# Two FFN units planned with the mixer, and the FFN's normalised activations moved from VectorE to ScalarE and GpSimd

## The chip, the core and the metric

The kernel runs on one core of one Trainium2 chip. The metric is the device time of one execution in microseconds (us), as the median of several runs. Five engines work side by side, each with its own queue of instructions that is worked off in order: TensorE (PE, with its weight loads shown apart as PEld), VectorE (DVE), ScalarE (ACT), GpSimd (POOL) and SyncE (SP, which here issues the DMAs).

## What is computed

Two pre-normalised residual layers and a last norm, for 512 tokens of width 1024. Layer 0's mixer has stick-breaking and native-sparse attention heads, layer 1's has forgetting attention. Each layer ends in a gated MLP (called FFN below) with a causal convolution of width 3 over its activation branch, and 2816 hidden channels:

```python
def rmsnorm(x, g):
    x32 = x.astype(jnp.float32)
    y = x32 * lax.rsqrt(jnp.mean(x32 * x32, axis=-1, keepdims=True) + NORM_EPS)
    return y.astype(x.dtype) * g

def conv_glu_ffn(h, w_in, conv_w, conv_b, w_out):
    a, b = jnp.split(h @ w_in, 2, axis=-1)
    a = conv(a, conv_w) + conv_b          # causal, width 3, each channel by itself
    return (jax.nn.silu(a) * b) @ w_out

for layer in range(DEPTH):
    x = x + mixer(rmsnorm(x, attn_norm[layer]))
    x = x + conv_glu_ffn(rmsnorm(x, ffn_norm[layer]), ...)
return rmsnorm(x, final_norm)
```

## The kernel before

All activations lie transposed, with channels on the 128 partitions and the 512 tokens along the free dimension, so X is eight tiles X[0] to X[7]. Each fp32 operand is split in a high part and a low part, and a product of 128 input channels is three matmuls: high weights by high activations, low weights by high activations, high weights by low activations. The weights are split on the fly: a DMA brings the tile wraw, ScalarE copies it to whi (rounding it), and VectorE subtracts, giving wlo. The pairs whi and wlo have two buffers each, and so has wraw.

**A mixer's end.** The last output projections add their products to X (VectorE, line 541). For each finished X[m], Mixer.feed (line 545) gives the FFN's input: ScalarE makes XH[m] = X[m] times the norm's gain g, VectorE makes the low part XL[m], ScalarE squares X[m], and GpSimd adds the square to ACC. The factor 1/rms (tile rstd) is left out of XH and XL. It is known only when all of ACC is, and it is multiplied in when a product is taken out of PSUM.

**An FFN's start** (ffn, line 1121). A unit is 128 of the columns of w_in: eight steps of three matmuls, one step for each XH[k], XL[k]. The first six column pairs (PLAIN = 6, so twelve units) are plain: for pair c, unit 2c gives the activation branch a, unit 2c+1 gives b. VectorE takes a and b out of PSUM with a product by rstd, makes two of the convolution's three taps, the product by silu, and the low part GL of the result; ScalarE makes the first tap, silu, and the high part GH. norm() makes rstd: a matmul of ACC with ones (written below as stats), then VectorE, ScalarE twice and VectorE three times.

The other 16 pairs go by a scheme with seven products in place of eight (function seven, tiles named s, t and o in PSUM). It needs sums and differences of normalised activations, which sums(k) makes for k = 0 to 3: VectorE writes x[k] = X[k] * g * rstd and x[k+4] likewise (line 1245, tile gh), GpSimd makes four half-wide sums d1 and d3 from them (tile gl), and ScalarE and VectorE split them into b1, b2, t1 and t3. No product of seven can start before all of these are there.

**What sets the order.** A mixer and an FFN are each written as a list of jobs for a planner (class Plan, line 104). A job has an engine, a cost in us written by hand, jobs it depends on, a priority, and buffers that it takes and gives back. The planner simulates the engines with those costs: of the jobs of an engine that could start within 0.03 us of the earliest, the one with the lowest priority number goes first. The order that comes out is each engine's program order, and nothing on the chip changes it. On VectorE, taking products out of PSUM has priority 1, gates 1.1, weight splitting 1.2, sums 2 to 2.3 and XL 4. A unit's matmuls have 100 and more.

The mixer's plan ends with its last projection. After it, ffn issues the weights of its first two units (line 1131, outside of the plan) and starts a second plan whose engines come free at times written by hand (line 1132). In that plan unit 0 runs to its end, the matmul stats is issued behind unit 0's seventh step (lines 1222 and 1223), and unit 1 follows. Plain units alternate between two PSUM banks (mm_bank), and two more banks, t and o, are kept for the sevens.

Of the kernel before, what the change touches and what calls it, by code (L numbers as in the profile page):

```python
# [10 lines left out]
F32 = mybir.dt.float32  # L11
# [7 lines left out]
P = 128  # L19
# [74 lines left out]

class Job:


    def __init__(self, eng, cost, fn, deps, prio, take, give, lat):
        self.eng, self.cost, self.fn, self.deps = eng, cost, fn, deps
        self.prio, self.take, self.give, self.lat = prio, take, give, lat  # L100
        self.end, self.got = None, []


class Plan:
# [13 lines left out]
    def add(self, eng, cost, fn, *deps, prio=5.0, take=(), give=(), lat=0.0):  # L118
        j = Job(eng, cost, fn, [d for d in deps if d is not None], prio, take, give, lat)
        self.jobs.append(j)  # L120
        return j

    def _when(self, j):
# [8 lines left out]
        for n in set(j.take):  # L132
            b = sorted(self.bufs[n])[:j.take.count(n)]
            if len(b) < j.take.count(n):
                return None
            t = max(t, b[-1][0] + self.LAG)
        return t

    def run(self):
        while self.jobs:  # L140
# [14 lines left out]
            for n in j.take:  # L155
# [5 lines left out]
            for n in j.give:  # L161

                for n, i in [(n, 0)] if isinstance(n, str) else [g for g in n.got if g[0] == "b"]:
# [6 lines left out]
def trunk(ctx, tc, A):  # L170
# [17 lines left out]
    names = dict(t=2, o=3)  # L188
# [5 lines left out]
    def hand_over(plan):  # L194

        order = [i for _, i in sorted(plan.bufs["b"])]
        turns.clear()
        turns.extend(order[:2])
        names.update(t=order[2], o=order[3])
# [52 lines left out]
    def warm():  # L252
# [3 lines left out]
        ps = bank(names["t"], "t")  # L256
# [94 lines left out]
    def finish(fp, src, oh, ol):  # L351
# [48 lines left out]
        for b in range(2):  # L400
            for m in ms:
                tag = ("mm", "mm", "t", "o")[m - ms[0]]
                ps = mm_bank() if tag == "mm" else bank(names[tag], tag)
# [42 lines left out]
    class Mixer:  # L446


        def __init__(self, plan, qp, ap):
            self.plan, self.qp, self.ap = plan, qp, ap  # L450
            self.seq, self.prev_load, self.prev_v = 0, None, None
            self.copied = [None, None]
            self.vs = []

        def bank(self, name, n=0):
            return bank([i for k, i in self.plan.now.got if k == "b"][n], name)
# [88 lines left out]
        def feed(self, m, layer, j):  # L545
# [15 lines left out]
            def scaled():  # L561
# [4 lines left out]
            self.plan.add("DVE", 0.75, lambda: dve.scalar_tensor_tensor(XL[m], X[m], g, XH[m].bitcast(F32), op0=ALU.mult, op1=ALU.subtract),  # L566
                          a, prio=4)
            a = self.plan.add("ACT", 0.62, square, j, prio=4.5, take=("sq",))
            self.plan.add("POOL", 1.35, add, a, prio=4, give=("sq",))
# [232 lines left out]
    def layer0():  # L802
        with ExitStack() as es:
# [71 lines left out]
            def new_o():  # L875
                o = bank(names["o"], "o")
# [233 lines left out]
            part(range(4, 8), 6, 2, (oj[7],), last)  # L1110
            inorder[0] = True
            plan.run()
            inorder[0] = False
            hand_over(plan)
# [6 lines left out]
    def ffn(layer, nl, final):  # L1121
# [7 lines left out]
        with ExitStack() as es:  # L1129
            fp = es.enter_context(tc.tile_pool(name=f"fp{layer}", bufs=2))  # L1130
            first = [weights(A["wfi"][layer, u], [P, NK, P]) for u in range(2)]
            plan = Plan(dict(PE=0.0, ACT=2.6, DVE=2.6, POOL=4.9, SP=-5.0), dict(PE=0.03), wraw=2, wb=2, wo=2, w=2, mm=2, s=2, t=1, o=1,
                        a=2, tt=1, b=2, g=10, sr=2, slot=NK, sq=2)
            plan.bufs["w"], plan.bufs["slot"] = [], []
# [34 lines left out]
            def gated(c, box, *deps):  # L1169
# [7 lines left out]
                GJ[c] = add("DVE", 0.69, lambda: dve.tensor_sub(GL[c], box["b"], GH[c].bitcast(F32)), j, prio=p, give=("b",))  # L1177


            def norm():  # L1180
# [12 lines left out]
                acc = add("POOL", 0.0, lambda: None, prio=0)  # L1193
                j = add("PE", 0.5, stats, acc, prio=0, take=("s",))
# [10 lines left out]
            def plain(c, root):  # L1205
                box = {}
                ps = []
                for u in range(2):
                    w = M.weights(A["wfi"][layer, 2 * c + u], [P, NK, P]) if c else (dict(h=first[u][0], l=first[u][1]), None)
                    lastu = (c, u) == (PLAIN - 1, 1)  # L1210
                    bx, j = {}, None
                    for k in range(NK):
                        def step(k=k, w=w, bx=bx):
                            if k == 0:
                                bx["ps"] = mm_bank()
# [17 lines left out]
                j = add("DVE", 0.69, fa, ps[0][1], root[0], prio=1, take=("a",), give=("mm",))  # L1233
# [447 lines left out]
```

## Time and profile before

| what | value |
|---|---|
| median of 3 runs | 1252.84 us (1252.83 to 1253.6) |
| the profiled execution's own time | 1250.37 us |
| its span in the profile | 1248.2 us |
| TensorE busy | 1223.1 us, 98% of the span |
| VectorE, ScalarE, GpSimd busy | 923.0, 631.6 and 230.2 us |
| first FFN's matmuls begin, sevens begin | 289.78 us, 360.55 us |
| second FFN's matmuls begin, sevens begin | 882.10 us, 951.53 us |

A row of the timeline has the start, the duration in us, the engine, the operation, the tile written and the tiles read, the shape, and how often it comes in a row; in brackets stands how long the engine sat idle before it and who ended that. Durations of neighbours overlap by some hundredths, so the distance between starts is what an instruction costs its engine. All instructions go through one helper (L88), so they are told apart by tile names.

### The profile page before, as it was taken

The page shows a single profiled execution, that of the slowest core. Times are in us where ns is not written, and L with a number is a line of the kernel's source. Part 1 is how long each engine was busy: PE and PEld are TensorE (multiplying, and loading weights), DVE is VectorE, ACT ScalarE, POOL GpSimd, SP SyncE. Part 2 cuts the span into 40 slices and gives each one's busy share as a digit, 9 for nine tenths or more (in the row PEclk, how much of TensorE's full clock was granted, in tenths as well). Part 3 has the DMA queues.
Part 4 walks back from the last instruction along what each step waited for, and adds up shares of the span by engine and source line. Part 5 has one row for each costly group of instructions (what it writes and reads, how often), then busy time and mean ns, then how long its engine had stood idle before and what let it go on. Part 6 is the DMA issues. An engine that isn't in the chain of part 4 may idle for free.

```text
span 1248.2 us, 19483 instructions
## 1 busy us (share of the span) xinstructions
PE 1223.1 (98%) x7484; PEld 1038.2 (83%) x7484; DVE 923.0 (74%) x1576; ACT 631.6 (51%) x1148; POOL 230.2 (18%) x272
## 2 busy tenths in 40 slices
PE   8999999999999999999999999999999999999997
PEld 5887866677889999999887878777788999999986
DVE  6668757658998799888762443444899889988875
ACT  6676537745554445444452664542555445444452
POOL 0000104413510001000030452310441000100011
PEclk9999999999999999999999999999999999999999
DMA  6314141012251342323233553312225124232421
GB/s 213 118 35 124 52 130 52 18 51 83 86 169 41 113 132 81 114 72 137 78 109 105 188 160 98 110 52 85 85 86 168 64 94 148 72 108 82 131 66 68
DMA packets 51420, 124.18 MB, mean 99 GB/s; under 512 B 6064, under 2 KB 17584, under 8 KB 51328
## 3 DMA queue, kind: packets, MB, share of 16 engines
q1 hardware_dynamic: 49808, 121.35, 30.0%
q10 hardware_dynamic: 1520, 1.59, 0.4%
q8 instruction: 59, 0.97, 0.3%
q14 instruction: 33, 0.27, 0.1%
HBM read 119.28 MB, written 2.13 MB: 97 GB/s over the span
## 4 chain that ended last, share of the span: by engine, by line
PE 88%; DVE 6%; ACT 1%; issue 1%; SPq 1%; DMA 1%; POOL 1%; DVEq 0%; ACTq 0%; POOLq 0%
PE mm L88 50%; PE s L88 20%; PE t L88 10%; PE o L88 7%; SPq L88 1%; DVE x L88 1%; DVE xl L88 1%; DVE wlo L88 1%; POOL e L88 1%; DVE e L88 1%; ACT whi L88 0%; DMA x<-x 0%; DVE sxl L88 0%; ACT xh L88 0%; DMA swp<-q 0%
## 5 line engine op out<-in xcount | busy, mean ns | idle before, releaser
L88 PE MATMUL mm<-xl,whi 128*128 128x512 f32 x424 | 166.2, 392 | 5.0 <-DVE xl L88 4.9
L88 PE MATMUL mm<-xh,whi 128*128 128x512 f32 x424 | 169.5, 400 | 1.4 <-ACT xh L88 1.4
L88 PE MATMUL mm<-xh,wlo 128*128 128x512 f32 x424 | 165.7, 391 | 1.1 <-DVE wlo L88 1.1
L88 DVE TENSOR_TENSOR wlo<-wraw,whi 128x1024 fp32r<-128x1024 f32 (+3 forms) x83 | 105.8, 1275 | 55.0 <-ACT whi L88 54.7
L88 ACT CAST whi<-wraw 128x1024 fp32r<-128x1024 f32 (+3 forms) x83 | 83.8, 1010 | 99.3 <-PE mm L88 73.8
L88 POOL TENSOR_TENSOR sr<-wraw,wb 128x512 f32<-128x512 f32 x32 | 47.4, 1481 | 462.8 <-DVE sr L88 288.1
L88 PE MATMUL mm<-gh,wlo 128*128 128x512 f32 x332 | 130.1, 392 | 0.0
L88 PE MATMUL mm<-gh,whi 128*128 128x512 f32 x332 | 130.0, 392 | 0.0
L88 PE MATMUL mm<-gl,whi 128*128 128x512 f32 x332 | 129.2, 389 | 0.0
L88 ACT CAST sxh<-sr 128x512 fp32r<-128x512 f32 x128 | 76.4, 617 | 83.5 <-DVE sr L88 54.2
L88 DVE TENSOR_TENSOR x<-x,mm 128x512 f32<-128x512 f32 (+2 forms) x104 | 70.0, 674 | 63.9 <-PE mm L88 63.5
L88 PEld LDWEIGHTS mm<-xl,whi 128*128 128x128 f32 x424 | 79.8, 188 | 24.6 <-DVE xl L88 7.5
L88 POOL TENSOR_SCALAR e<-e,dn 128x128 f32<-128x128 f32 (+3 forms) x128 | 72.3, 586 | 148.7 <-DVE dn L88 148.6
L88 PEld LDWEIGHTS mm<-xh,whi 128*128 128x128 f32 x424 | 79.9, 189 | 21.4 <-issue 3.3
L88 DVE TENSOR_TENSOR sxl<-sr,sxh 128x512 fp32r<-128x512 f32 x128 | 95.0, 760 | 2.7 <-ACT sxh L88 1.9
L88 PEld LDWEIGHTS mm<-xh,wlo 128*128 128x128 f32 x424 | 80.0, 189 | 18.1 <-DVE wlo L88 1.7
L88 ACT ACTIVATE tt<-a,conv 128x512 f32<-128x512 f32 x44 | 36.0, 817 | 114.5 <-DVE a L88 114.5
L88 ACT ACTIVATE e<-e,nm 128x256 f32<-128x256 f32 (+3 forms) x128 | 70.8, 556 | 43.9 <-DVE nm L88 40.9
L88 DVE SCALAR_TENSOR_TENSOR tt<-a,conv,tt 128x510 f32<-128x510 f32 x88 | 72.6, 826 | 8.4 <-ACT tt L88 7.2
L88 PEld LDWEIGHTS mm<-gl,whi 128*128 128x128 f32 x332 | 62.4, 188 | 13.3
L88 PE MATMUL s<-t3l,sxh 128*128 128x256 f32 x256 | 72.4, 283 | 0.0
L88 PE MATMUL s<-t3h,sxl 128*128 128x256 f32 x256 | 72.4, 283 | 0.0
(248 smaller groups left out, 3372.4 us busy)
## 6 DMA issues: line engine op xcount, KB each, us to landing
wraw<-wfi SPq DMA_DIRECT2D x56, 512.0 KB
wb<-wfi SPq DMA_DIRECT2D x32, 512.0 KB
wraw<-wu SPq DMA_DIRECT2D x31, 512.0 KB
wo<-wfo SPq DMA_DIRECT2D x32, 384.0 KB
wo<-wfo SPq DMA_DIRECT2D x28, 320.0 KB
wraw<-wo SPq DMA_DIRECT2D x16, 512.0 KB
wraw<-wv SPq DMA_DIRECT2D x10, 512.0 KB
cb<-cd SPq DMA_DIRECT2D x8, 512.0 KB
```

What stands on the lines that cost most here:

```text
L88: r = f(*a, **k)
```

## The change

1. **Two units in the mixer's plan.** ahead(M, layer), called behind the last projections and before the mixer's plan runs, adds the weights and the steps of the FFN's units 0 and 1 as jobs. Each step depends on the job that makes XL[k]. Their priority, 100 and the running number of their weights, lies behind that of the projections.
2. **What is handed over.** hand_over() passes on when each engine, weight buffer and PSUM bank comes free in the mixer's plan and when ACC is complete, and the FFN's plan starts from these. It no longer contains units 0 and 1; stats is its first matmul, so it comes behind both units.
3. **Banks.** Units 0 and 1 keep the banks they had in the mixer's plan. The plain units after them take whichever of the four (mm, t, o) comes free first.
4. **The normalised activations.** x[c] = X[c] * g is made by ScalarE, which needs no rstd, and GpSimd multiplies it by rstd in place. VectorE does nothing for it. x[k+4] is scaled only after x[k] has been multiplied.
5. The written cost of GpSimd's add to ACC goes from 1.35 to 1.4 us.

```diff
+    def ahead(M, layer):
+        first = []
+        for u in range(2):
+            w = M.weights(A["wfi"][layer, u], [P, NK, P])
+            bx, j = {}, None
+            for k in range(NK):
+                def step(k=k, w=w, bx=bx):
+                    if k == 0:
+                        bx["ps"] = M.bank("mm")
+                    h, l = w[0]["h"][:, k], w[0]["l"][:, k]
+                    mm(bx["ps"], h, XH[k], k == 0, False)
+                    mm(bx["ps"], l, XH[k], False, False)
+                    mm(bx["ps"], h, XL[k], False, k == NK - 1)
+                j = M.plan.add("PE", 0.69, step, w[1], M.xl[k], j, prio=100 + M.seq, take=("b",) if k == 0 else (), give=("w",) if k == NK - 1 else ())
+                bx.setdefault("job", j)
+            first.append((bx, j))
+        return first
...
-            first = [weights(A["wfi"][layer, u], [P, NK, P]) for u in range(2)]
-            plan = Plan(dict(PE=0.0, ACT=2.6, DVE=2.6, POOL=4.9, SP=-5.0), dict(PE=0.03), wraw=2, wb=2, wo=2, w=2, mm=2, s=2, t=1, o=1,
-                        a=2, tt=1, b=2, g=10, sr=2, slot=NK, sq=2)
-            plan.bufs["w"], plan.bufs["slot"] = [], []
+            plan = Plan(left["free"], dict(PE=0.03), wb=2, wo=2, s=2, a=2, tt=1, bb=2, g=10, sr=2, sq=2)
+            plan.bufs.update(w=left["w"], wraw=left["wraw"], slot=[], mm=[], t=left["b"][:1], o=left["b"][1:])
...
-                acc = add("POOL", 0.0, lambda: None, prio=0)
-                j = add("PE", 0.5, stats, acc, prio=0, take=("s",))
+                j = add("PE", 0.5, stats, left["acc"], prio=0, take=("s",))
...
-                        j = add("PE", 0.685, step, w[1], j, prio=100 + c, take=("mm",) if k == 0 else (), give=give)
-                        if (c, u, k) == (0, 0, NK - 2):
-                            root.append(next(nj))
+                        j = add("PE", 0.685, step, w[1], j, prio=100 + c, give=give, alts=("mm", "t", "o") if k == 0 else ())
...
                 def norm(c):
                     x[c] = g_tile("gh", F32)
-                    dve.scalar_tensor_tensor(x[c], X[c], ng[:, nl - 1, c:c + 1], rstd, op0=ALU.mult, op1=ALU.mult)
+                    act.activation(x[c], X[c], AF.Copy, scale=ng[:, nl - 1, c:c + 1])
...
-                j = add("DVE", 0.75, lambda: norm(k), root[0], prio=p, take=("g",))
-                j = add("DVE", 0.75, lambda: norm(k + H), j, prio=p, take=("g",))
-                eng, e, cost = (pool, "POOL", 0.74) if True else (dve, "DVE", 0.42)
+                eng, e, cost = pool, "POOL", 0.74
+                j = None
+                for c in (k, k + H):
+                    j = add("ACT", 0.73, lambda c=c: norm(c), j, prio=p, take=("g",))
+                    j = add(e, 1.4, lambda c=c: eng.tensor_mul(x[c], x[c], rstd), j, root[0], prio=p)
```

More of the change, by code (lines that the diff above doesn't have):

```diff
@@ L116, in __init__, with add @@
         self.jobs = []
-    def add(self, eng, cost, fn, *deps, prio=5.0, take=(), give=(), lat=0.0):
-        j = Job(eng, cost, fn, [d for d in deps if d is not None], prio, take, give, lat)
+    def add(self, eng, cost, fn, *deps, prio=5.0, take=(), give=(), lat=0.0, alts=()):
+        j = Job(eng, cost, fn, [d for d in deps if d is not None], prio, take, give, lat, alts)
         self.jobs.append(j)
@@ L136, in _when @@
             t = max(t, b[-1][0] + self.LAG)
+        if j.alts:
+            b = [(min(self.bufs[n]), n) for n in j.alts if self.bufs[n]]
+            if not b:
+                return None
+            j.choice = min(b)[1]
+            t = max(t, min(b)[0][0] + self.LAG)
         return t
@@ L154, in run @@
             self.jobs.remove(j)
-            for n in j.take:
+            for n in (*j.take, j.choice) if j.alts else j.take:
                 b = min(self.bufs[n])
@@ L192, in mm_bank, with done, hand_over @@
         return bank(turns[-1], "mm")
[L194 to L199, printed above, removed]
+    left = {}
+    def done(t):
+        j = Job("", 0.0, None, [], 0, (), (), 0.0)
+        j.end = t
+        return j
+    def ahead(M, layer):
[15 more added lines that the diff above has]
+        return first
+    def hand_over(M, first):
+        plan = M.plan
+        t = plan.free["PE"]
+        left["free"] = {e: f - t for e, f in plan.free.items()}
+        left["acc"] = done(M.acc.end - t)
+        left["w"] = [(f - t, i) for f, i in plan.bufs["w"]]
+        left["wraw"] = [(f - t, i) for f, i in plan.bufs["wraw"]]
+        left["b"] = sorted((f - t, i) for f, i in plan.bufs["b"])
+        left["first"] = []
+        for bx, j in first:
+            d = done(j.end - t)
+            d.got = [("mm", i) for n, i in bx["job"].got if n == "b"]
+            left["first"].append((dict(bx, job=d), d))
     def s_banks():
@@ L255, in warm @@
         pool.memset(z, 0.0)
[L256 removed]
+        ps = bank(2, "t")
         for n in range(12):
@@ L452, in __init__ @@
             self.copied = [None, None]
+            self.xl, self.acc = {}, None
             self.vs = []
         def bank(self, name, n=0):
-            return bank([i for k, i in self.plan.now.got if k == "b"][n], name)
+            return bank([i for k, i in self.plan.now.got if k in BANKS][n], name)
         def weights(self, src, shape, place=None, token="w", split=None):
@@ L1113, in layer0 @@
             inorder[0] = False
-            hand_over(plan)
+            hand_over(M, first)
     layer0()
@@ L1208, in plain @@
                 for u in range(2):
-                    w = M.weights(A["wfi"][layer, 2 * c + u], [P, NK, P]) if c else (dict(h=first[u][0], l=first[u][1]), None)
+                    if c == 0:
+                        ps.append(left["first"][u])
+                        continue
+                    w = M.weights(A["wfi"][layer, 2 * c + u], [P, NK, P])
                     lastu = (c, u) == (PLAIN - 1, 1)
@@ L1345, in seven @@
                 j = product(1, "p2", "t2", "t")
-                u = take("DVE", 0.42, first_b, j, cp_, take=("b",), give=("t",))
+                u = take("DVE", 0.42, first_b, j, cp_, take=("bb",), give=(j,))
                 j = product(2, "p1", "t1", "s")
@@ L1349, in seven @@
                 j = product(3, "p4", "b22", "o")
-                c12 = take("DVE", 0.42, lambda: dve.tensor_sub(av(HI), box[3], bv(HI)), j, v, give=("o",))
+                c12 = take("DVE", 0.42, lambda: dve.tensor_sub(av(HI), box[3], bv(HI)), j, v, give=(j,))
                 j = product(4, "p3", "t3", "s")
@@ L1353, in seven @@
                 j = product(5, "a2", "b21", "t")
-                c11 = take("DVE", 0.42, lambda: dve.tensor_add(av(LO), av(LO), box[5]), j, u, give=("t",))
+                c11 = take("DVE", 0.42, lambda: dve.tensor_add(av(LO), av(LO), box[5]), j, u, give=(j,))
                 t = gate(c, box, c11, c12)
@@ L1582, in layer1 @@
             inorder[0] = False
-            hand_over(plan)
+            hand_over(M, first)
     layer1()
```

38 lines of the change are left out of this document (21 added, 17 removed).

## The prediction

> **What bounds the kernel now.** I read the page first: busy times, then the chain of work that ended last.
>
> ```profile
> span 1248.2 us, 19483 instructions
> ...
> PE 1223.1 (98%) x7484; PEld 1038.2 (83%) x7484; DVE 923.0 (74%) x1576; ACT 631.6 (51%) x1148; POOL 230.2 (18%) x272
> ...
> PE 88%; DVE 6%; ACT 1%; issue 1%; SPq 1%; DMA 1%; POOL 1%; DVEq 0%; ACTq 0%; POOLq 0%
> ```
>
> TensorE bounds the whole. What an edit can win is the 2% in which it stands still or runs at a lower clock; what it can lose is any place where another engine has nothing to spare. So the second view is a table of the two stretches that the change touches, from about the moment rstd is there to the end of the plain units (window, its length, then busy us of PE, PEld, DVE, ACT and POOL, the granted clock, DMA).
>
> ```profile
> 304.00:360.00 56.00, 56.00 (x249) 46.32 (x248) 53.93 (x72) 31.87 (x47) 20.45 (x16) 1.00 0.36 121
> 896.00:952.00 56.00, 56.00 (x250) 46.02 (x249) 54.45 (x72) 32.17 (x48) 20.44 (x16) 1.00 0.36 118
> ```
>
> TensorE is full here, but VectorE is too: 53.93 and 54.45 of 56 us. The average of 74% hides that. The third view, the waits of the second stretch, shows how near it is (who waits for whom: us in total, times, longest):
>
> ```profile
> PEld mm L88 <- DVE wlo L88: 0.4, 1, 0.4
> ```
>
> A weight load already waits for a wlo. VectorE can lose next to nothing in the plain phase before TensorE stands.
>
> The fourth view is the timeline of the junction from mixer to FFN, first of layer 0, then of layer 1, with the chain's pieces (start, us, what, count) around stats.
>
> ```profile
> 290.75 1.30 POOL L88 TENSOR_TENSOR acc<-acc,sq 128x512 f32<-128x512 f32 x1 [0.59 <-ACT sq L88]
> ...
> 291.23 1.36 DVE L88 SCALAR_TENSOR_TENSOR xl<-x,ng,xh 128x512 fp32r<-128x512 f32 x1
> ...
> 293.11 2.08 DVE L88 TENSOR_TENSOR wlo<-wraw,whi 128x1024 fp32r<-128x1024 f32 x1
> ...
> 294.09 0.39 PE L88 MATMUL mm<-xh,wlo 128*128 128x512 f32 x1
> ...
> 295.12 2.41 DVE L88 SCALAR_TENSOR_TENSOR xl<-x,ng,xh 128x512 fp32r<-128x512 f32 x2
> ...
> 296.92 0.50 PE L88 MATMUL mm<-xl,whi 128*128 128x512 f32 x1 [2.44 <-DVE xl L88]
> ```
> ```profile
> 886.40 0.39 PE L88 MATMUL mm<-xh,wlo 128*128 128x512 f32 x1
> ...
> 889.24 0.50 PE L88 MATMUL mm<-xl,whi 128*128 128x512 f32 x1 [2.44 <-DVE xl L88]
> ...
> 895.03 0.69 DVE L88 SCALAR_TENSOR_TENSOR rstd<-rs_u,rstd 128x512 f32<-128x512 f32 x1
> ```
> ```profile
> 298.14 1.71 PE s L88 x2
> 299.85 60.70 PE mm L88 x264
> ```
> ```profile
> 890.44 0.86 PE s L88 x2
> ...
> 891.30 60.23 PE mm L88 x264
> ```
> ```profile
> 298.00:302.00 4.00, 4.00 (x10) 2.51 (x9) 1.82 (x2) 2.34 (x3) 0.00 (x0) 0.58 0.02 8
> ```
> ```profile
> 890.00:894.00 4.00, 4.00 (x17) 2.97 (x17) 2.25 (x3) 2.37 (x3) 0.00 (x0) 1.00 0.10 35
> ```
>
> Unit 0 waits for XL[6] behind VectorE's queue. A matmul follows the last after 60.23 / 264 = 0.228 us, so the wait costs 296.92 - 294.09 - 0.23 = 2.60 us in layer 0, and 2.61 us in layer 1. In layer 0 the granted clock then falls to 0.58: stats takes 1.71 us against 0.86, and the 264 matmuls of units 1 to 11 take 60.70 against 60.23, so 0.85 + 0.47 = 1.32 us more. A unit is 60.23 / 11 = 5.48 us.
>
> **Part one: the two units in the mixer's plan.** Removed: at most the two waits and the slow stretch, 2 x 2.6 + 1.32 = 6.5 us. No matmul is added. But the units do not get between the projections: their priority number is higher, their weights need buffers that the last projections give back, and XL[k] needs X[k]. They can only fill each other's waits. Unit 1 can start when the wlo of 293.11 is done, at 295.19; XL[6] is done at 296.9. So of 2.6 us about 0.9 stays, unless the queue changes. I worked the planner's order out by hand from the written costs: it expects XL[6] within 0.02 us of the moment TensorE is free, too near to call, and if unit 0's seventh step goes first, TensorE stands in it as before. Bounds 0 and 2.6 us per FFN; I take the middle, 1.3. Of the slow stretch, bounds 0 and 1.32, I take half, 0.65, since the shorter wait may or may not bring it about. Together 3.25 us won. Below nothing these terms cannot go, as the same matmuls stand behind the same work.
>
> The DMAs of the two units stay behind the projections' on SP; no matmul of the junction waits for one now. The free choice of four banks is worth nothing here: in 56 of 56 us TensorE waits for no bank.
>
> What it moves is stats, which comes behind both units. Before, in layer 1, unit 1 ends at 891.30 + 5.48 = 896.78 and rstd is done at 895.72: 1.06 us before unit 2 begins. After, stats ends when unit 2 begins, and rstd comes 895.72 - 891.30 = 4.42 us later. Everything on VectorE that needs rstd starts 5.5 us later as TensorE sees it, in a stretch in which VectorE is full.
>
> **Part two: the normalised activations.** VectorE loses eight instructions per FFN, ScalarE gains eight like those of XH, GpSimd eight as wide as the adds to ACC.
>
> ```profile
> L88 DVE SCALAR_TENSOR_TENSOR gh<-x,ng,rstd 128x512 f32<-128x512 f32 x8 | 5.8, 744 | 0.0
> ```
> ```profile
> 293.22 0.72 ACT L88 ACTIVATE xh<-x,ng 128x512 fp32r<-128x512 f32 x1 [0.54 <-DVE x L88]
> ```
>
> VectorE is relieved of 5.8 us. ScalarE's 8 x 0.72 = 5.8 us cost nothing: it is busy 31.87 of 56 us and half of the scaling needs no rstd. If that cover were gone, GpSimd would wait, not TensorE. GpSimd's 8 x 1.30 = 10.4 us look free too, but these rows say otherwise (the first two with GpSimd idle, the next three with it at work; then groups of the stretch from 304 to 360 us with busy us and mean ns, and two tiles with min/median/max ns):
>
> ```profile
> 306.74 1.53 DVE L88 SCALAR_TENSOR_TENSOR tt<-a,conv,tt 128x510 f32<-128x510 f32 x2
> 308.18 1.22 DVE L88 TENSOR_TENSOR wlo<-wraw,whi 128x1024 fp32r<-128x1024 f32 x1
> ```
> ```profile
> 313.55 1.76 DVE L88 TENSOR_TENSOR wlo<-wraw,whi 128x1024 fp32r<-128x1024 f32 x1
> 315.24 2.37 DVE L88 SCALAR_TENSOR_TENSOR tt<-a,conv,tt 128x510 f32<-128x510 f32 x2
> ```
> ```profile
> 314.19 1.73 POOL L88 TENSOR_TENSOR gl<-gl,gh 128x256 f32<-128x256 f32 x1
> ```
> ```profile
> L88 DVE TENSOR_TENSOR wlo<-wraw,whi 128x1024 fp32r<-128x1024 f32 x9 | 11.7, 1303 | 0.0
> L88 DVE SCALAR_TENSOR_TENSOR tt<-a,conv,tt 128x510 f32<-128x510 f32 x6 | 6.4, 1064 | 0.0
> L88 DVE SCALAR_TENSOR_TENSOR tt<-a,conv,tt 128x511 f32<-128x511 f32 x6 | 5.9, 990 | 0.2
> ```
> ```profile
> L88 POOL TENSOR_TENSOR gl<-gh x16: 742/1240/2382, 305.8 to 937.8; 128x256 f32<-128x256 f32 x16
> ```
> ```profile
> L88 DVE TENSOR_TENSOR b1l<-gh,b1h x4: 409/684/959, 317.5 to 350.1; 128x256 fp32r<-128x256 f32 x4
> ```
>
> An instruction of VectorE with two operands in SBUF and one of GpSimd wait for each other: wlo takes 1.76 us in place of 1.22, the two taps 2.37 in place of 1.53, and GpSimd's half-wide sum 1.73 in place of 0.74. Over the stretch VectorE pays 9 x (1.303 - 1.22) = 0.75 us in wlo, 6.4 + 5.9 - 6 x 1.53 = 3.1 in taps and 4 x (0.684 - 0.409) = 1.1 in b1l, 5.0 us, for 16 x 0.74 = 11.9 us of GpSimd's work: 0.42 us each. Inside a group of sums, where they follow each other closely, wlo and taps pay 0.54 + 0.84 = 1.38 for three sums of 2.23 us: 0.62 each. In the new plan they all follow closely, since GpSimd no longer waits for VectorE between groups: 8 x 1.4 + 16 x 0.74 = 23 us of written cost in one run behind rstd.
>
> The sum is made at unit 7, where by the written costs VectorE's queue has three pairs behind it. Distances between starts:
>
> ```profile
> 342.80 1.22 DVE L88 TENSOR_TENSOR wlo<-wraw,whi 128x1024 fp32r<-128x1024 f32 x1
> 343.94 0.68 DVE L88 TENSOR_TENSOR gl<-b,gh 128x512 fp32r<-128x512 f32 x1
> 344.54 0.68 DVE L88 TENSOR_TENSOR t3l<-gl,t3h 128x512 fp32r<-128x512 f32 x1
> 345.14 0.74 DVE L88 SCALAR_TENSOR_TENSOR gh<-x,ng,rstd 128x512 f32<-128x512 f32 x1
> 345.81 0.68 DVE L88 TENSOR_TENSOR a<-mm,rstd 128x512 f32<-128x512 f32 x1
> 346.41 1.44 DVE L88 TENSOR_TENSOR wlo<-wraw,whi 128x1024 fp32r<-128x1024 f32 x1
> ```
> ```profile
> 346.03 0.74 POOL L88 TENSOR_TENSOR gl<-gh,gl 128x256 f32<-128x256 f32 x1 [6.03 <-DVE gh L88]
> ```
>
> The read from PSUM (a) and the sum of 346.03 overlap and neither is longer for it. From rstd to the wlo of unit 7 stand six reads from PSUM (0.60 each), four wlo (1.14), three tap pairs (1.44), five products and GL parts (0.60), and of the splits two b1l and three of full width (together 2.5): 18.0 us. Unit 7 begins five units behind unit 2, so 5 x 5.48 - 4.42 = 23.0 us are there, and 5.0 are left for waits. In front of that wlo GpSimd's order has seven products and eleven sums, 7 x 1.30 + 11 x 0.74 = 17.3 us. At 0.42 VectorE waits 7.3 us and is 2.3 late; at 0.62 it waits 10.7 and is 5.7 late; if every us counts but the 3.6 spent reading PSUM, 13.7, it is 8.7 late. Behind the wlo stands TensorE, which has no other job in its order. Lost time is not regained, since TensorE cannot go faster than 5.48 us a unit. I take 0.55, between the two measured shares and nearer to that of the dense group: 9.5 us, 4.5 late per FFN. Nothing at all is the lower end, if fewer of GpSimd's instructions get in.
>
> **The sum.** 2 x 4.5 - 3.25 = 5.75 us longer. The profiled execution of 1250.37 us would take 1256.1; it lies 2.5 us below the median of 1252.84, which becomes 1258.6.
>
> **The rivals.** A difference of 0.2%, 2.5 us, is about what a measurement can tell from no change.
>
> *Relief wins (0.27).* VectorE's eight instructions are gone, and its waits reach no wlo in time to matter: this decides from 5.0 / 17.3 = 0.29 us of waiting per us of GpSimd downwards. For it: a read from PSUM does not wait, and GpSimd, itself held up, may do fewer than 18 instructions before unit 7. Against it: both measured shares are above 0.29. The gains are left, 3.25 to 6.5 us: 1246.3 to 1249.6, about 1249.
>
> *A draw (0.13).* VectorE is late by 0.4 to 2.9 us per FFN, which gives the gains back: about 1252.8.
>
> *As forecast (0.42).* Late by 3 to 6 us per FFN: 1255.6 to 1261.6.
>
> *The units change nothing (0.05).* The planner keeps unit 0's seventh step in front, the waits and the slow stretch stay, and part two costs its 9 us: 1261.8.
>
> *Every microsecond counts (0.13).* Each instruction of GpSimd holds VectorE for its whole length unless VectorE reads PSUM: 2 x 8.7 - 3.25 = 14.1 us, 1267. For it: the taps let one sum in between the two. Against it: the share of 0.62 inside a group. The Trainium skill's page "SBUF — State Buffer" (section "SBUF: two separate sides") has this as a rule: the pair of ports that the two engines share is an exclusive lock, held for the whole instruction, and the loser is blocked outright. By that rule the offload exchanges 5.8 us for up to 10.4; the rows agree that they exclude each other.
>
> The Trainium skill's "TensorE: Matmul & The Clock Gate" (section "What's actually happening") says that the clock halves after an idle window of some 3.4 us that runs free of the kernel. By the rows here equal waits did it once in two, for 1.32 us; new waits for wlo could do so again, which lies inside the range.
>
> **How the numbers follow.** Faster 0.27, within 0.2% 0.13, slower 0.42 + 0.05 + 0.13 = 0.60. The range runs from 1247, in the midst of the first case, to 1266, just under the last.
>
> **What would show it.** Right: waits of TensorE for wlo of some us between units 4 and 8 of each FFN; taps and wlo stretched while GpSimd multiplies; stats behind unit 1 and rstd 4.4 us after it; the wait for XL at the junction shortened, not gone. Wrong: TensorE full through the plain units; VectorE under 50 of 56 us there; GpSimd's products spread over the phase and not in one run; or a wait for t1 or t3 where the sevens begin.

## The result, and the profile after

The changed kernel takes 1266.97 us (median of 4 runs, 1266.06 to 1267.48) against 1252.84 (4 runs, 1249.77 to 1253.6): the ratio is 1.0117, with a 95% interval of 1.0098 to 1.0135. It is slower by 14.1 us, beyond the top of the range (1266) and 8.4 us above the forecast.

The page of the kernel after (the line of the busy times, and the shares in the chain of work that ended last):

```profile
span 1265.7 us, 19465 instructions
...
PE 1227.9 (97%) x7484; PEld 1039.9 (82%) x7484; DVE 927.0 (73%) x1560; ACT 639.8 (51%) x1164; POOL 256.9 (20%) x288
...
PE 84%; DVE 9%; issue 2%; ACT 2%; SPq 1%; DMA 1%; POOL 1%; DVEq 0%; ACTq 0%; POOLq 0%
```

The edit is there: 16 instructions fewer on VectorE, 16 more on ScalarE and on GpSimd. Yet VectorE is busy for 4.0 us longer, with fewer instructions, and its share of the chain goes from 6% to 9%. The same two windows as before (length, busy us of PE, PEld, DVE, ACT and POOL, granted clock, DMA):

```profile
304.00:360.00 56.00, 49.03 (x202) 39.15 (x201) 54.01 (x60) 31.58 (x49) 32.38 (x24) 0.94 0.31 102
896.00:952.00 56.00, 48.97 (x196) 38.35 (x197) 48.86 (x52) 30.20 (x46) 33.52 (x25) 0.94 0.25 79
```

VectorE is as busy as before in the first (54.01 against 53.93), but does 60 instructions in place of 72. GpSimd works 12 us longer, and TensorE, full before, loses 7 us in each window. (The second FFN starts 8 us later than before, so its window lies that much earlier in the stage.) TensorE's waits say for what (us in total, times, longest):

```profile
PE mm L88 <- DVE wlo L88: 11.3, 7, 3.3
PE mm L88 <- ACT whi L88: 3.7, 2, 1.8
PE mm L88 <- DVE xl L88: 2.4, 2, 1.2
```

Before, the first was 1.1 us, once, the second was absent, and the third was 4.9. (That 1.1 is a wait at 15.62 us, at the program's start, which both kernels have; in the FFNs no matmul waited for wlo.) The timeline of TensorE shows where, in layer 0 and then in layer 1 (in brackets the idle time before the matmul, and who ended it):

```profile
295.44 0.50 PE L88 MATMUL mm<-xl,whi 128*128 128x512 f32 x1 [1.19 <-DVE xl L88]
...
315.14 0.50 PE L88 MATMUL mm<-xh,wlo 128*128 128x512 f32 x1 [0.73 <-DVE wlo L88]
...
327.47 0.50 PE L88 MATMUL mm<-xh,wlo 128*128 128x512 f32 x1 [1.16 <-DVE wlo L88]
...
334.83 0.50 PE L88 MATMUL mm<-xh,whi 128*128 128x512 f32 x1 [1.82 <-ACT whi L88]
...
338.58 0.80 PE L88 MATMUL mm<-xh,wlo 128*128 128x512 f32 x1 [3.25 <-DVE wlo L88]
```
```profile
935.48 0.50 PE L88 MATMUL mm<-xh,whi 128*128 128x512 f32 x1 [1.83 <-ACT whi L88]
...
939.23 0.79 PE L88 MATMUL mm<-xh,wlo 128*128 128x512 f32 x1 [3.24 <-DVE wlo L88]
```

The junction's wait is cut by half, as said. In exchange units 4, 6 and 7 wait for their weights: 0.73 + 1.16 + 1.82 + 3.25 = 6.96 us of idle time in layer 0, and 6.88 in layer 1. Counted from start to start less 0.228, as the junction's wait was counted, it is 7.7 us in layer 0. Behind the longest wait the matmuls come slowly (windows around unit 7's wait of layer 0, then the one behind that of layer 1):

```profile
334.00:338.00 4.00, 0.50 (x1) 0.19 (x1) 4.00 (x4) 3.29 (x6) 3.92 (x4) 0.86 0.02 4
338.00:342.00 4.00, 3.42 (x8) 2.77 (x9) 4.00 (x5) 0.39 (x1) 3.38 (x3) 0.50 0.41 131
342.00:346.00 4.00, 4.00 (x15) 3.19 (x15) 3.96 (x7) 2.67 (x5) 0.00 (x0) 0.78 0.11 19
```
```profile
940.00:944.00 4.00, 4.00 (x11) 3.11 (x10) 4.00 (x6) 0.72 (x1) 2.04 (x2) 0.50 0.41 131
```

The granted clock is 0.50 for 4 us. The matmul that begins at 341.73 lies in two of these windows, so 8 + 15 - 1 = 22 matmuls begin from 338.58 to 346.00, and this is the last of them:

```profile
345.90 0.40 PE L88 MATMUL mm<-xh,wlo 128*128 128x512 f32 x1
```

Their 21 steps take 7.32 us; at 0.228 us each they would take 4.79. So 2.5 us more, and nearly the same in layer 1.

The chain's pieces around stats in layer 0 (start, us, what, count):

```profile
297.13 5.97 PE mm L88 x25
303.11 0.86 PE s L88 x2
303.97 4.79 PE mm L88 x21
```

Between stats and the end of unit 2 at 308.76 stand 21 matmuls, and not 24. The timeline has 51 matmuls from the start of unit 0 to stats, 48 of them of units 0 and 1. So stats is not the first matmul of the FFN's plan: the first step of unit 2 runs ahead of it, and likewise in layer 1.

Now VectorE and GpSimd in layer 0, from rstd to unit 7's wlo:

```profile
307.70 0.69 DVE L88 SCALAR_TENSOR_TENSOR rstd<-rs_u,rstd 128x512 f32<-128x512 f32 x1
...
310.58 2.82 DVE L88 SCALAR_TENSOR_TENSOR tt<-a,conv,tt 128x510 f32<-128x510 f32 x2 [0.28 <-ACT tt L88]
313.33 1.75 DVE L88 TENSOR_TENSOR wlo<-wraw,whi 128x1024 fp32r<-128x1024 f32 x1
315.44 0.79 DVE L88 TENSOR_TENSOR b<-b,tt 128x512 f32<-128x512 f32 x1 [0.36 <-ACT tt L88]
...
319.04 2.92 DVE L88 SCALAR_TENSOR_TENSOR tt<-a,conv,tt 128x510 f32<-128x510 f32 x2
...
323.91 0.68 DVE L88 TENSOR_TENSOR a<-mm,rstd 128x512 f32<-128x512 f32 x1
...
325.11 2.31 DVE L88 TENSOR_TENSOR wlo<-wraw,whi 128x1024 fp32r<-128x1024 f32 x1
...
330.75 2.37 DVE L88 SCALAR_TENSOR_TENSOR tt<-a,conv,tt 128x510 f32<-128x510 f32 x2
...
336.78 1.74 DVE L88 TENSOR_TENSOR wlo<-wraw,whi 128x1024 fp32r<-128x1024 f32 x1
```
```profile
308.61 4.25 POOL L88 TENSOR_TENSOR gh<-gh,rstd 128x512 f32<-128x512 f32 x3 [12.08 <-DVE rstd L88]
...
324.55 5.73 POOL L88 TENSOR_TENSOR gh<-gh,rstd 128x512 f32<-128x512 f32 x3
...
340.21 1.17 POOL L88 TENSOR_TENSOR gl<-gl,gh 128x256 f32<-128x256 f32 x1
```
```profile
333.21 0.63 ACT L88 ACTIVATE tt<-tt 128x512 f32<-128x512 f32 x1 [4.38 <-DVE tt L88]
333.74 1.03 ACT L88 CAST whi<-wraw 128x1024 fp32r<-128x1024 f32 x1
```

GpSimd's products and sums follow each other from 308.61 to 341.4, 32.8 us for 23 us of written cost. A wlo or a pair of taps that meets them is stretched, most of all the pair at 319.04, by 1.39 us (2.92 against 1.53). The wlo of unit 7 ends at 338.52, 30.1 us behind rstd. Its whi is late too: in ScalarE's queue it stands behind a silu, and that waited 4.38 us for VectorE's taps.

Where the 17.5 us between the two spans lie: from the first FFN's first matmul to its sevens it is 78.74 us in place of 70.77 (+7.97), in the second 78.71 in place of 69.43 (+9.28). The rest of the program adds 0.3 us in all; its largest single piece is a wait of 0.78 us for k at 689.73, in the second mixer.

### The profile page after: what moved, and what is told of

Its sections match the earlier page's. It is cut to its first block, busy times and chain, and to the rows that moved or that the text cites. A ratio compares the mean times of both kernels' runs of the same rounds, so it can differ in the third digit from the quotient of the medians.

```text
span 1265.7 us, 19465 instructions
## 1 busy us (share of the span) xinstructions
PE 1227.9 (97%) x7484; PEld 1039.9 (82%) x7484; DVE 927.0 (73%) x1560; ACT 639.8 (51%) x1164; POOL 256.9 (20%) x288
## 4 chain that ended last, share of the span: by engine, by line
PE 84%; DVE 9%; issue 2%; ACT 2%; SPq 1%; DMA 1%; POOL 1%; DVEq 0%; ACTq 0%; POOLq 0%
PE mm L88 58%; PE s L88 20%; PE o L88 3%; PE t L88 3%; SPq L88 1%; DVE wlo L88 1%; DVE tt L88 1%; POOL e L88 1%; DVE x L88 1%; DVE b L88 1%; DVE xl L88 1%; DVE e L88 1%; ACT whi L88 1%; DMA swp<-q 0%; DMA x<-x 0%
## 5 line engine op out<-in xcount | busy, mean ns | idle before, releaser
L88 DVE TENSOR_TENSOR wlo<-wraw,whi 128x1024 fp32r<-128x1024 f32 (+3 forms) x83 | 108.5, 1307 | 56.4 <-ACT whi L88 56.1
L88 PE MATMUL mm<-b2h,sxl 128*128 128x256 f32 x256 | 72.8, 284 | 0.5
```

Source lines behind the costliest of these rows:

```text
L88: r = f(*a, **k)
```

## The experiments

The theory (**reads**): where VectorE has no slack, each product of GpSimd that reads SBUF holds up VectorE's instructions with two operands in SBUF. Rivals: **late rstd** (the 5.5 us by which VectorE's queue starts later are the loss, whoever makes the activations), **the packed run** (only the lack of gaps between GpSimd's instructions hurts), and **GpSimd's time** (the products only make the sums late). Each ratio is to the kernel before, timed together with it (its median lay between 1250.48 and 1251.20 us beside these runs). Costs below are worked out from the ratios at 1251 us; by its own ratio the change costs 14.6 us. The intervals are 2.4 to 5.8 us wide, so a difference of 1 or 2 us between two runs is not told apart from none. "after:" above a diff says that it is against the changed kernel.

| run | median, us | ratio, 95% interval |
|---|---|---|
| part one alone | 1260.96 | 1.0073 (1.0056 to 1.0090) |
| part two alone | 1265.18 | 1.0112 (1.0093 to 1.0130) |
| after, statistics early | 1266.87 | 1.0123 (1.0106 to 1.0140) |
| after, no products | 1251.46 | 1.0002 (0.9991 to 1.0013) |
| part one, statistics early | 1251.12 | 1.0004 (0.9995 to 1.0014) |
| after, memsets for products | 1252.00 | 1.0015 (1.0004 to 1.0026) |
| after, products spread | 1273.96 | 1.0191 (1.0173 to 1.0209) |
| part one early, unit 2 planned | 1261.25 | 1.0084 (1.0068 to 1.0101) |
| after, measured costs | 1278.45 | 1.0219 (1.0203 to 1.0236) |
| after, half on VectorE | 1269.40 | 1.0146 (1.0123 to 1.0169) |
| part one early, unit 2 ahead | 1250.40 | 0.9999 (0.9986 to 1.0013) |
| after, GpSimd reads nothing | 1246.46 | 0.9967 (0.9954 to 0.9980) |
| part one, sums read nothing | 1253.01 | 1.0013 (1.0001 to 1.0026) |
| after, half the products left out | 1258.09 | 1.0055 (1.0039 to 1.0071) |

### The parts by themselves

Part one alone is the changed kernel with VectorE's normalised activations; part two alone is the kernel before with the offload.

```diff
after:
-                    act.activation(x[c], X[c], AF.Copy, scale=ng[:, nl - 1, c:c + 1])
+                    dve.scalar_tensor_tensor(x[c], X[c], ng[:, nl - 1, c:c + 1], rstd, op0=ALU.mult, op1=ALU.mult)
...
-                    j = add(e, 1.4, lambda c=c: eng.tensor_mul(x[c], x[c], rstd), j, root[0], prio=p)
```

> The changed kernel with the normalised activations made by VectorE again, as before; the two planned units, the banks and stats behind both units stay. Theory A (GpSimd's eight products, run in one row behind rstd, hold up VectorE's queue): the waits for wlo in units 4 to 7, 7 to 8 us per FFN, and the slow clock after them shrink to at most 3 us per FFN; the shortened wait at the junction stays won: 1250 to 1256 us. Theory B (rstd comes 5.5 us too late, since stats stands behind both units, and who makes the products hardly matters): the waits stay, 1262 to 1267 us.

> The kernel before with the normalised activations made by ScalarE and GpSimd, and nothing else: units 0 and 1 outside of the mixer's plan, stats between them. Theory A: VectorE's queue up to unit 7 still needs some 29 us against 28 that are there now, so TensorE waits for wlo by 1 to 4 us per FFN, with a slow clock where a wait is long: 1255 to 1262 us. Theory B: rstd is in time, so the relief of VectorE wins: 1250 to 1253 us.

Part one alone costs 9.1 us where it was to win (its time lies between the ranges of the two theories), part two alone 14.0 (more than either theory gave), and both together 14.6. The parts do not add up, and the theory had put all of the loss down to part two. Part two alone has rstd some 1 us before unit 2 begins, as the kernel before has, and still TensorE waits for VectorE in the plain units, 0.51 + 0.48 + 2.18 + 0.68 + 0.90 = 4.75 us in layer 0. The timeline of TensorE in part one alone has no wait for weights among the plain units but one of 0.20; the others stand where the sevens' products begin (two are shown; one of 0.66 us for gl lies between them):

```profile
359.98 0.50 PE L88 MATMUL mm<-gh,wlo 128*128 128x512 f32 x1 [1.45 <-DVE wlo L88]
...
371.38 0.50 PE L88 MATMUL mm<-gh,wlo 128*128 128x512 f32 x1 [1.99 <-DVE wlo L88]
```

### The statistics early

stats and the steps of rstd become jobs of the mixer's plan, between the two units, with priority 0; once with the offload, once with part one alone.

```diff
+        j = add("PE", 0.9, stats, M.acc, prio=0, take=("s",))
+        a = add("DVE", 0.5, start, j, prio=0, take=("sq", "sq"))
...
+        left["root"] = add("DVE", 0.75, lambda: dve.scalar_tensor_tensor(r, ps["u"], 1.5, r, op0=ALU.add, op1=ALU.mult), j, prio=0,
+                           give=("sq", "sq"))
...
-            root = [next(nj)]
+            root = [left["root"]]
```

> The changed kernel with stats and the steps that make rstd as jobs of the mixer's plan, so that they run as soon as ACC is complete, in the midst of unit 1. The offload stays. Theory A: the run of GpSimd's products starts some 5 us earlier, and so do VectorE's jobs; the waits fall to 1 to 3 us per FFN: 1251 to 1258 us. Theory B: all waits for wlo go, the junction's gain is left: 1248 to 1250 us. If neither is the cause (for instance whi behind silu in ScalarE's queue): above 1262 us.

> Part one of the change alone (VectorE makes the normalised activations again), with stats and the steps to rstd as jobs of the mixer's plan, so that rstd comes in the midst of unit 1 and not 4.4 us after stats behind unit 1. If the 10 us that part one alone costs come from the late rstd: they go, and the junction's 1.2 us per FFN and the slow clock's 1.3 us are won: 1246 to 1250 us. If they come from another step of part one (the banks, the handed over times, the weights in the mixer's plan): 1258 to 1261 us.

With the offload rstd is done 0.5 us after unit 2 begins in place of 6.1, and nothing is won, which neither theory gave. The planner makes another order here, so this does not weigh the late rstd by itself. What it shows is that an early rstd is no remedy: waits for wlo of 1.26, 3.46, 0.86 and 1.72 us stand in the plain units of layer 0. None is for whi, so whi behind a silu is not the cause there either. With part one alone, again in a new order, 8.6 of its 9.1 us go. But nothing is won over the kernel before. The steps of rstd now stand ahead of unit 2's weights, and TensorE waits there:

```profile
305.29 0.50 PE L88 MATMUL mm<-xh,wlo 128*128 128x512 f32 x1 [1.30 <-DVE wlo L88]
```

Two runs went after that wait. The first puts unit 2's weights into the mixer's plan, the second leaves the plan alone and only issues those two instructions ahead of rstd's.

```diff
+        left["w2"] = M.weights(A["wfi"][layer, 2], [P, NK, P])
...
-                    w = M.weights(A["wfi"][layer, 2 * c + u], [P, NK, P])
+                    w = left["w2"] if (c, u) == (1, 0) else M.weights(A["wfi"][layer, 2 * c + u], [P, NK, P])
```

> The version of part one with early stats, and the weights of unit 2 as jobs of the mixer's plan too. In that version the gain at the junction (1.2 us per FFN) is given back where unit 2 starts: its whi and wlo stand behind the steps to rstd in ScalarE's and VectorE's queues, and TensorE waits 1.3 us. If that is all: the wait goes, 1248 to 1250 us, 1.5 to 3.5 us under the kernel before. If another step of VectorE comes late instead: 1250 to 1252 us.

```diff
+        a2 = add("ACT", 0.0, hi2, s2, first[0][1], prio=-1)
+        add("DVE", 0.0, lambda: dve.tensor_sub(w2["l"], w2["w"], w2["h"].bitcast(F32)), a2, prio=-1)
```

> Part one with VectorE's activations and early statistics, its plan left as it is; only the instructions that make the weights of unit 2 (one cast by ScalarE, one subtraction by VectorE) are issued ahead of the three steps of rstd instead of behind them. If what ate the junction's gain is that these two stood behind the rstd steps in their queues, the wait of 1.30 us per FFN at unit 2 goes and nothing takes its place: 1247.5 to 1250 us. If that wait only covers a lateness of VectorE that shows up elsewhere, the time stays at about 1251.

In both the wait at unit 2 is gone. In the first the planner makes another order and new waits come (1.75 us for gl at 366.15, 1.86 for sxl at 454.91), so that it costs 10.5 us, more than either theory gave. In the second the order stays, a wait of 0.43 us for wlo shows at 331.50, and 1250.40 is no gain. Where the rest of the junction's gain goes there stays open: no single wait accounts for it.

### What it is about the products

All products left out, in the same order; then each replaced by two memsets of the same tile, which read nothing (constants stand for the activations).

```diff
after:
-                    j = add(e, 1.4, lambda c=c: eng.tensor_mul(x[c], x[c], rstd), j, root[0], prio=p)
+                    j = add(e, 1.4, lambda c=c: None, j, root[0], prio=p)
```

> The changed kernel in the same planned order, but GpSimd's eight products by rstd per FFN are left out, so the sums are made of activations that are not normalised. Only 10.4 us of GpSimd's work per FFN is missing. Theory A: VectorE's taps and wlo are stretched by the half-wide sums alone, the waits fall to 0 to 3 us per FFN: 1249 to 1256 us. Theory B: VectorE starts as late as in the changed kernel, 1261 to 1267 us.

```diff
after:
-                    j = add(e, 1.4, lambda c=c: eng.tensor_mul(x[c], x[c], rstd), j, root[0], prio=p)
+                    j = add(e, 1.4, lambda c=c: [eng.memset(x[c], 0.5) for _ in range(2)], j, root[0], prio=p)
```

> The changed kernel in the same planned order, with each of GpSimd's eight products per FFN replaced by two memsets of the same tile, which occupy GpSimd for about as long (a memset of this size takes 0.52 us, two 1.05) but read nothing from SBUF; the sums are then made of constants. If GpSimd's reads and VectorE's two-operand reads exclude each other (theory A as I hold it): VectorE is not stretched by the memsets, TensorE waits as without products, 1249 to 1255 us. If it is GpSimd's being busy that delays things, by its queue or by writes: 1260 to 1267 us.

Without the products 14.4 us go, with memsets 12.8. A memset of 128x512 takes GpSimd 0.527 us, so two of them occupy it for 1.05 us, against 1.30 for a product: four fifths of the time on GpSimd cost 1.6 us if nothing is read, and the two intervals overlap. (The memsets need not wait for rstd, so GpSimd can begin a little earlier.) And in the changed kernel no engine waits for GpSimd from 304 to 360 us. So GpSimd's time is at most a small part of the cause. What is left without products are waits for wlo of 2.9 us over both FFNs, in layer 0 these:

```profile
332.19 0.50 PE L88 MATMUL mm<-xh,wlo 128*128 128x512 f32 x1 [1.07 <-DVE wlo L88]
...
338.29 0.50 PE L88 MATMUL mm<-xh,wlo 128*128 128x512 f32 x1 [0.36 <-DVE wlo L88]
```

The next run asks whether the half-wide sums' reads make them:

```diff
after:
-                    j = add(e, 1.4, lambda c=c: eng.tensor_mul(x[c], x[c], rstd), j, root[0], prio=p)
-                s1 = add(e, cost, lambda: eng.tensor_sub(x["d1"][:, LO], x[k][:, LO], x[k][:, HI]), j, prio=p)
+                    j = add(e, 1.4, lambda c=c: [eng.memset(x[c], 0.5) for _ in range(2)], j, root[0], prio=p)
+                s1 = add(e, cost, lambda: [eng.memset(x["d1"][:, LO], 0.5) for _ in range(2)], j, prio=p)
...
```

> The changed kernel in its own order, with all of GpSimd's products and also its half-wide sums replaced by writes of a constant, two for each, which read nothing (the outputs are constants, so this part of the computation is left out). If GpSimd's reads against VectorE's are everything, TensorE's waits for weights go except for what the junction keeps: 1248 to 1250 us. If what remained without the products' reads comes from the late statistics, it stays: 1251 to 1252 us.

1246.46 us, 4.1 below the kernel before and less than either theory gave: what the change wins shows once nothing reads against VectorE. (The kernel before has the sums' reads too, but in its FFNs no matmul waits for wlo.) The same window in this kernel, then its groups in that window (busy us, mean ns), and the groups of the changed kernel in the same window:

```profile
304.00:360.00 56.00, 56.00 (x248) 46.06 (x247) 47.84 (x69) 36.98 (x57) 16.22 (x46) 1.00 0.36 124
```
```profile
L88 DVE TENSOR_TENSOR wlo<-wraw,whi 128x1024 fp32r<-128x1024 f32 x9 | 11.0, 1217 | 0.0
L88 DVE SCALAR_TENSOR_TENSOR tt<-a,conv,tt 128x511 f32<-128x511 f32 x6 | 4.5, 752 | 0.2
```
```profile
L88 DVE TENSOR_TENSOR wlo<-wraw,whi 128x1024 fp32r<-128x1024 f32 x9 | 13.1, 1455 | 0.0
L88 DVE SCALAR_TENSOR_TENSOR tt<-a,conv,tt 128x511 f32<-128x511 f32 x5 | 5.4, 1077 | 0.2
```

TensorE is full again, VectorE needs 47.84 us, and wlo and taps take what they take alone (1.217 and 0.752 us), though GpSimd works beside them for 16.22 us. With the reads they take 1.455 and 1.077. rstd is done 6.1 us after unit 2 begins, as late as in the changed kernel, and the time is the best of all. So with the offload it is the reads that make the loss, and a late rstd without them costs TensorE no wait for weights. GpSimd's time is matched only roughly here: it is busy for half as long as in the changed kernel.

### How the loss grows

Half of the products left out, in the same order:

```diff
after:
-                    j = add(e, 1.4, lambda c=c: eng.tensor_mul(x[c], x[c], rstd), j, root[0], prio=p)
+                    j = add(e, 1.4, lambda c=c: eng.tensor_mul(x[c], x[c], rstd) if k < 2 else None, j, root[0], prio=p)
```

> The changed kernel in its own order, with the products of the last two of the four activation tiles left out (GpSimd does 4 products per FFN instead of 8; this part of the computation is left out). All products cost 15.5 us. If each product costs the same, about 1.0 us, this gives 1258 to 1260 us; if what counts is that the first ones meet the queue ahead of unit 7's weights, nearly all stays lost: 1263 to 1266 us; if there is slack for some, nearly all is gained: 1252 to 1255 us.

The waits of layer 0 in that kernel:

```profile
316.45 0.50 PE L88 MATMUL mm<-xh,wlo 128*128 128x512 f32 x1 [0.73 <-DVE wlo L88]
...
328.23 0.50 PE L88 MATMUL mm<-xh,wlo 128*128 128x512 f32 x1 [0.60 <-DVE wlo L88]
...
336.14 0.50 PE L88 MATMUL mm<-xh,wlo 128*128 128x512 f32 x1 [2.13 <-DVE wlo L88]
```

Now four kernels have the same order on every engine and differ only in what GpSimd does in place of sums and products. Counting 0.74 us for a sum and 1.30 for a product, over both FFNs: nothing read, 0.9967 of the kernel before; sums alone (23.7 us), 1.0002; half of the products too (34.1 us), 1.0055; all (44.5 us), 1.0117. At 1251 us the steps are 4.4, 6.6 and 7.8 us, or 0.18, 0.64 and 0.75 us of the whole time per us of GpSimd's reading. Each step is uncertain by 2 to 3 us, so 0.64 and 0.75 are not told apart, but the first is clearly less: the first us meet what slack VectorE has, and then each costs some two thirds of its length. The slow clock is in these steps. In the profiled executions it came in no FFN without products, in layer 1 alone with half of them, and in both with all.

Part one alone with its sums reading nothing:

```diff
part one alone:
-                s1 = add(e, cost, lambda: eng.tensor_sub(x["d1"][:, LO], x[k][:, LO], x[k][:, HI]), j, prio=p)
+                s1 = add(e, cost, lambda: [eng.memset(x["d1"][:, LO], 0.5) for _ in range(2)], j, prio=p)
...
```

> Part one alone (VectorE makes the activations, as in the kernel before, statistics late), with GpSimd's half-wide sums replaced by writes of a constant that read nothing (so the output projection is left out in part). If part one's 10 us come from the sums' reads taking VectorE's last margin, the time falls to 1254 us or less. If they come from the late rstd alone, with VectorE full by itself, it stays at 1257 to 1261 us.

7.5 of part one's 9.1 us go, in an unchanged order. An early rstd, in a new one, took away 8.6. So neither alone makes part one's loss: the sums' reads and a late rstd have to come together in a full VectorE, and relief on either side takes most of it away.

### Other orders

Three runs tried to keep the offload and lay it out better: the products of each activation tile wait for the splits of the tile before; costs in the plan nearer to the measured ones; and half of the activations back on VectorE.

```diff
after:
+                    j = add(e, 1.4, lambda c=c: eng.tensor_mul(x[c], x[c], rstd), j, root[0], *TJ[-1:], prio=p)
```

> The changed kernel with GpSimd's products for k made to wait for the splits of k - 1, so that its work is spread over the plain phase as before the change and not in one run behind rstd. The amount of work is the same. If the run is what hurts: the worst wait, at unit 7, and with it the slow clock go, 1253 to 1259 us. If the amount of exclusion against a late rstd is what hurts, wherever it falls: the waits move to later units and stay, 1261 to 1267 us.

> The changed kernel with the same instructions, but the planner is told the durations that the trace shows under contention: 1.8 us for a product on GpSimd (written 1.4), 1.2 for a half-wide sum (0.74), 1.2 for a tap on VectorE (0.72). If the loss comes from an order that is wrong about the chip: the splits move back in VectorE's queue, wlo comes in time, 1253 to 1259 us. If it is the amount of work that excludes each other: the waits only move, 1261 to 1270 us.

```diff
after:
-                j = add("DVE", 0.72, lambda: tap(2), j, prio=p)
+                j = add("DVE", 1.2, lambda: tap(2), j, prio=p)
...
-                eng, e, cost = pool, "POOL", 0.74
+                eng, e, cost = pool, "POOL", 1.2
...
-                    j = add(e, 1.4, lambda c=c: eng.tensor_mul(x[c], x[c], rstd), j, root[0], prio=p)
+                    j = add(e, 1.8, lambda c=c: eng.tensor_mul(x[c], x[c], rstd), j, root[0], prio=p)
```

> The changed kernel with half of the normalised activations (k = 2 and 3) made by VectorE again and half by ScalarE and GpSimd. Each product on GpSimd costs about 1 us by the runs so far (16 products left out: 15.5 us less), and each one that VectorE makes instead costs 0.6 (part one alone stands 9.5 us above the same without products, which leaves them out altogether). By amounts it lies in the midst between part one alone and the changed kernel: 1262 to 1265 us. If the run of 24 instructions is what hurts, half of it hurts less than half: 1254 to 1260 us.

```diff
after:
+                    if k >= 2:
+                        j = add("DVE", 0.75, lambda c=c: norm_dve(c), j, root[0], prio=p, take=("g",))
+                        continue
```

All three have a higher median than the changed kernel and than any theory gave; with half on VectorE the interval overlaps that of the changed kernel (1.0098 to 1.0135). Spread, the waits leave the early units and stand at the end of the plain phase instead:

```profile
371.53 0.50 PE L88 MATMUL mm<-gl,whi 128*128 128x512 f32 x1 [2.01 <-DVE gl L88]
...
378.89 0.50 PE L88 MATMUL mm<-gh,wlo 128*128 128x512 f32 x1 [2.50 <-DVE wlo L88]
```

So gaps between the products are no remedy. That the packed run plays no part is not shown, since the planner made another order here. The last run shows what a new plan does to a size. With half of the products left out in the old order the time is 6.9 us above the kernel before; with that half on VectorE (8 instructions of 0.74 us over both FFNs) and everything planned anew it is 18.3. In layer 0 the additional waits lie between 356 and 375 us and at 455.92 (1.86 us, with the slow clock behind it), where the changed kernel has none. So a size is safe only from runs in an unchanged order. None of the kernels that compute everything beats the kernel before.

## Why the prediction was right or wrong

**Right: what bounds, and the direction.** VectorE was full in the plain phase and had nothing to give. The junction's wait went from 2.60 to 1.35 us per FFN (1.19 of it shown as idle), where 1.3 was taken as won; the slow stretch there went too, where half was taken. Together 2 x 1.25 + 1.32 = 3.8 us against 3.25, and the kernel in which nothing reads against VectorE wins 4.1. Both terms were middles between bounds, so that their sum came so near is luck. rstd is done 4.42 us after stats ends (303.11 + 0.86 to 307.70 + 0.69 us), as worked out. Units 4, 6 and 7 wait for their weights, as the list of signs had it. (A sign against it, VectorE under 50 of 56 us, shows in the second window above only because that window lies earlier in the stage; from 904 to 960 us VectorE is busy for 53.30.)

**Wrong: "I take 0.55 ... 9.5 us, 4.5 late per FFN".** This is the step that failed, in its size. In the trace 29.5 us in which VectorE is busy, and 0.64 us of its waits for ScalarE (0.28 and 0.36), which the sum left out, lie between rstd and the end of unit 7's wlo; the instructions in between are those that were counted. Against 18.0 without hindrance that is 11.5 us of waiting for GpSimd in place of 9.5. The share was not far off: in front of that wlo come 8 products and 13 sums, 8 x 1.30 + 13 x 0.74 = 20.0 us, so 11.5 / 20.0 = 0.57. But the count was: 20.0 us for 17.3. That a VectorE that is held up lets more of GpSimd's instructions in ahead, which holds it up further, would explain this; no run tests it by itself. The time that was there was too long as well: stats came behind three matmuls of unit 2, so 5 x 5.48 - 3 x 0.228 - 4.42 = 22.3 us and not 23.0. Late by 30.1 - 22.3 = 7.8 us in place of 4.5, and TensorE's waits at units 4, 6 and 7 are 7.7 from start to start.

**Wrong by omission: the clock.** That new waits could halve it was named and not priced ("lies inside the range"). It came in both FFNs, 2.5 us each, 5.0 in all, with a granted clock of 0.50 behind unit 7's two waits, between which TensorE was busy for only 0.50 us. The Trainium skill's page "TensorE: Matmul & The Clock Gate" (section "What's actually happening") says that the clock halves after an idle window of some 3.4 us. The runs agree with it only in part. A wait of 3.45 us left the clock at 1.00, and one of 2.15 us had 0.57 behind it (a matmul of layer 1 and the window behind it, first with the offload and statistics early, then with half of the products left out):

```profile
925.90 0.49 PE L88 MATMUL mm<-xh,wlo 128*128 128x512 f32 x1 [3.45 <-DVE wlo L88]
926.00:930.00 4.00, 4.00 (x18) 3.29 (x19) 4.00 (x4) 2.03 (x4) 3.92 (x4) 1.00 0.39 131
```
```profile
931.06 0.50 PE L88 MATMUL mm<-xh,wlo 128*128 128x512 f32 x1 [2.15 <-DVE wlo L88]
932.00:936.00 4.00, 4.00 (x13) 3.10 (x12) 4.00 (x7) 1.41 (x3) 0.75 (x1) 0.57 0.37 130
```

So the length of a wait alone did not decide it, and a sum made ahead could only have held a term between 0 and some 2.5 us per wait.

**The sum with what was measured.** 2 x (7.8 + 2.5) - 3.8 = 16.8 us. The spans differ by 17.5 and the times of the profiled executions by 17.1; the medians differ by 14.1, since the profiled execution before lies 2.5 us under its median and the one after 0.5 above. The 0.7 us between sum and spans are not assigned.

**Wrong: that the parts can be priced one by one.** By the prediction part one wins and part two costs 9. Part one alone costs 9.1, since VectorE, with the activations still on it, cannot take the late rstd while the sums read. In the changed kernel none of part one's waits ahead of the sevens are left, but the products' waits are more.

**The rivals.** "Relief wins" needed less than 0.29 us of waiting per us of GpSimd, and the trace has 0.57; the runs in an unchanged order give 0.64 and 0.75 us of the whole time once the slack is gone (the clock's fall included). "The units change nothing" is refuted by the junction. "Every microsecond counts" forecast the right time (1267) by a lateness of 8.7 us per FFN, of which 7.8 came, and without the clock. That is in part luck: it has 13.7 / 17.3 = 0.79 us of waiting per us of GpSimd, and the trace has 0.57, close to the forecast's own 0.55. The mechanism that the experiments show, GpSimd's reads holding up VectorE, is common to both. The Trainium skill's "SBUF — State Buffer" (section "Who interferes with whom") says that a VectorE instruction with two SBUF inputs contends with a GpSimd instruction that reads SBUF, not with one that only writes it: the memsets agree (wlo at 1.217 us beside them). The Trainium skill's "SBUF — State Buffer" (section "SBUF: two separate sides") says that the loser is blocked for the whole instruction. These rows show somewhat less: a wlo among GpSimd's sums paid 0.53 us (1.75 in place of 1.22) and one among its products 1.09 (2.31), against 0.74 and 1.30 us for a sum and a product.

## What to carry to other kernels

Before moving work from a full VectorE to an idle GpSimd, compare what VectorE is relieved of with GpSimd's whole reading time there: here 11.6 us of relief bought 20.8 us of reads, at 0.6 to 0.8 us of the kernel's time for each us once VectorE had no slack. To price one term, change it without letting a planner rebuild the order: leave the job and its cost in and empty its function. And when a wait of some us on TensorE is forecast, put the slow clock that may come behind it into the sum, at least as a range.

## What the runs showed of the hardware

GpSimd's memsets stretch nothing on VectorE: with 46 of them (16.22 us) from 304 to 360 us, wlo stayed at 1.217 us. And VectorE's reads of PSUM stayed at 0.68 to 0.69 us amid the products; only instructions with both tensor operands in SBUF were held up.
